# A row softmax on one core: an unrolled, framework-synchronised schedule rewritten with hand-made semaphores and hardware loops

## The chip, the cores and the metric

The kernel runs on one core of one Trainium2 chip. The engines that matter here are DVE (VectorE), ACT (ScalarE), Pool (GpSimd), SP (SyncE), PE's sequencer (no matrix work is done) and the core's 16 DMA engines. The metric is the device time of one execution in microseconds. A "span" is the time from the first to the last instruction in the profiled execution; it is about 1.8 us shorter than the time of the same execution. P below means the time from the first instruction of one tile to that of the next on DVE.

## The reference

```python
batch, seq, dim = 32, 512, 1024        # x: float32, temperature: 0.5
scaled  = x / temperature
shifted = scaled - np.max(scaled, axis=-1, keepdims=True)
exp_x   = np.exp(shifted)
out     = exp_x / np.sum(exp_x, axis=-1, keepdims=True)
```

These are 16384 rows of 1024 numbers: 67.1 MB in and 67.1 MB out. A tile is 128 partitions times 8 rows, 4 MB, and there are 16 tiles.

## The kernel before

Six tile buffers. SP loads, Pool stores, and a buffer is loaded again when its store has landed. The work goes in groups of 4 rows of a partition, two groups a tile. The framework makes the semaphores, and everything is unrolled.

```python
def maximum(g):      # DVE: row maxima of 4 rows, then bias = -scale * max
    nc.vector.tensor_reduce(out=top, in_=tiles[i][:, a : a + k, :], ..., op=extreme)
    nc.vector.tensor_scalar_mul(bias, in0=top, scalar1=-scale)

def exponential(g):  # ACT: exp(scale * x + bias) in place, and the sum of each row
    for b in range(k):
        nc.scalar.activation(tiles[i][:, a + b, :], tiles[i][:, a + b, :], Exp,
                             bias=bias[:, b : b + 1], scale=scale, accum_out=sums[:, b : b + 1])

def divide(g):       # DVE: 1 / sum, then one multiply a row
    nc.vector.reciprocal(recip, sums)
    for b in range(k):
        nc.vector.tensor_scalar_mul(...)
# ... cut ...
with tc.manual_schedule():
    for _ in range(BUFS):
        load()
    for g in range(len(groups) + 1):
        if g < len(groups):
            maximum(g)
            exponential(g)
        if g > 0:
            divide(g - 1)       # one group late
            store(g - 1)        # a 4 MB store at the end of each tile; then load()
```

While ACT does the exponentials of group g, DVE divides group g - 1 and then reduces group g + 1.

## Time and profile before

318.23 us, median of 3 runs (318.2 to 318.88).

| | before |
|---|---|
| span of the profiled execution | 316.9 us |
| DVE busy, ACT busy | 235.5 us, 149.6 us |
| DMA rate, 40 to 280 us | 432 to 434 GB/s |
| tile to tile (P), steps two to five / from the seventh on | 14.8 / 19.4 us (one of 20.2) |
| table loads on ACT | 1 |

The page of the kernel before. Each digit is a fortieth of the span, 7.9 us, in tenths busy; GB/s is what the DMA engines moved in it.

```profile
span 316.9 us, 639 instructions
DVE 235.5 (74%) x224; ACT 149.6 (47%) x257; POOL 8.8 (3%) x20
DVE  0399999999689494995949869496793967949710
DMA  8999999999999999999999999999999999999995
GB/s 331 409 451 414 385 459 422 438 436 422 455 405 455 409 459 405 455 422 438 434 426 451 409 455 411 455 414 447 426 434 435 426 451 409 451 418 447 430 414 232
```

The DMA row is full from the second slice to the last but one. DVE is full only at the start, while the six tiles loaded first are worked off; afterwards it has holes. The view of waits of the same kernel says what these holes are (engine, line, who was waited for: us in total, times, longest):

```profile
ACT xt L79 <- DVE recip L91: 119.5, 25, 8.1
DVE top L70 <- DMA xt<-in_x_dram: 62.8, 12, 13.1
DVE recip L91 <- ACT xt L79: 2.1, 2, 1.9
```

DVE's reduce waited 12 times for a load, and DVE waited almost never for ACT (2.1 us). The timeline of the second tile shows why (DVE's lines, and ACT's first exponential of the tile; the rest left out): the reciprocal at 29.84 works on the sums of the group before, which are long there.

```profile
25.31 4.41 DVE L70 TENSOR_REDUCE top<-xt 128x4 f32<-128x4096 f32 x1
29.76 0.17 DVE L73 TENSOR_SCALAR bias<-top 128x4 f32<-128x4 f32 x1
29.84 0.17 DVE L91 RECIPROCAL recip<-sums 128x4 f32<-128x4 f32 x1
29.96 1.15 ACT L79 ACTIVATE xt<-xt,bias 128x1024 f32<-128x1024 f32 x1 [3.03 <-DVE bias L73]
30.04 2.74 DVE L93 TENSOR_SCALAR xt<-xt,recip 128x1024 f32<-128x1024 f32 x4
32.70 4.41 DVE L70 TENSOR_REDUCE top<-xt 128x4 f32<-128x4096 f32 x1
```

So DMA bounds this kernel, and DVE and ACT have slack in every tile. First Pool's issue of the last two stores (the timeline: start us, us), then the DMA view of 280 to 325 us, each digit 1.1 us:

```profile
290.65 0.53 POOL L101 DMA_DIRECT2D out_dram<-xt  x1 [18.82 <-DVE xt L93]
302.90 0.53 POOL L101 DMA_DIRECT2D out_dram<-xt  x1 [11.72 <-DVE xt L93]
```

```profile
DMA  9999989989999999999859999999640000000000
GB/s 437 437 437 466 466 350 408 437 379 437 408 466 466 466 437 437 437 466 466 350 233 466 466 466 437 466 466 466 291 204 29 0 0 0 0 0 0 0 0 0
```

The last store is issued while the one before it is still moving, so the rate dips in one slice (233 GB/s) but no hole opens until the bytes are used up. By the landings in the trace, the last four stores end at 286.5, 296.1, 305.8 and 315.5 us: 9.7 us each, the time of 4 MB at the 432 to 434 GB/s of the middle.

Last, two lines of the page's groups (busy us, mean ns; idle before them):

```profile
L79 ACT ACTIVATE xt<-xt,bias 128x1024 f32<-128x1024 f32 x128 | 145.4, 1137 | 136.9 <-DVE recip L91 119.5
L79 ACT ACT_TABLE_LOAD x1 | 1.3, 1283 | 13.2 <-DMA xt<-in_x_dram 13.2
```

ACT loads the table of the exponential once, at the start, while DVE makes the first reduce.

### The profile page before, as it was taken

The page shows a single profiled execution, that of the slowest core. Times are in us where ns is not written, and L with a number is a line of the kernel's source. Part 1 is how long each engine was busy: PE and PEld are TensorE (multiplying, and loading weights), DVE is VectorE, ACT ScalarE, POOL GpSimd, SP SyncE. Part 2 cuts the span into 40 slices and gives each one's busy share as a digit, 9 for nine tenths or more (in the row PEclk, how much of TensorE's full clock was granted, in tenths as well). Part 3 has the DMA queues.
Part 4 walks back from the last instruction along what each step waited for, and adds up shares of the span by engine and source line. Part 5 has one row for each costly group of instructions (what it writes and reads, how often), then busy time and mean ns, then how long its engine had stood idle before and what let it go on. Part 6 is the DMA issues. An engine that isn't in the chain of part 4 may idle for free.

```text
span 316.9 us, 639 instructions
## 1 busy us (share of the span) xinstructions
DVE 235.5 (74%) x224; ACT 149.6 (47%) x257; POOL 8.8 (3%) x20
## 2 busy tenths in 40 slices
DVE  0399999999689494995949869496793967949710
ACT  0176666666526255361554606455163551635500
POOL 0000000000000000000000000000000000000000
DMA  8999999999999999999999999999999999999995
GB/s 331 409 451 414 385 459 422 438 436 422 455 405 455 409 459 405 455 422 438 434 426 451 409 455 411 455 414 447 426 434 435 426 451 409 451 418 447 430 414 232
DMA packets 4612, 134.25 MB, mean 424 GB/s; under 512 B 512, under 2 KB 512, under 8 KB 512
## 3 DMA queue, kind: packets, MB, share of 16 engines
q1 hardware_dynamic: 2304, 67.11, 49.5%
q0 software_dynamic: 2304, 67.11, 49.1%
q14 instruction: 4, 0.03, 0.0%
HBM read 67.11 MB, written 67.11 MB: 424 GB/s over the span
## 4 chain that ended last, share of the span: by engine, by line
issue 89%; DMA 4%; POOL 2%; POOLq 0%
DMA xt<-in_x_dram 4%; POOL out_dram L101 2%; POOLq L147 0%; POOLq L101 0%
## 5 line engine op out<-in xcount | busy, mean ns | idle before, releaser
L79 ACT ACTIVATE xt<-xt,bias 128x1024 f32<-128x1024 f32 x128 | 145.4, 1137 | 136.9 <-DVE recip L91 119.5
L70 DVE TENSOR_REDUCE top<-xt 128x4 f32<-128x4096 f32 x32 | 141.3, 4416 | 62.8 <-DMA xt<-in_x_dram 62.8
L93 DVE TENSOR_SCALAR xt<-xt,recip 128x1024 f32<-128x1024 f32 x128 | 87.7, 749 | 1.1
L79 ACT ACTIVATION_READ_ACCUMULATOR xt<-xt,bias 128x1 f32 x128 | 23.8, 186 | 0.0
L101 POOL DMA_DIRECT2D out_dram<-xt x16 | 8.6, 540 | 294.4 <-DVE xt L93 294.4
L79 ACT ACT_TABLE_LOAD x1 | 1.3, 1283 | 13.2 <-DMA xt<-in_x_dram 13.2
L91 DVE RECIPROCAL recip<-sums 128x4 f32<-128x4 f32 x32 | 5.5, 171 | 2.1 <-ACT xt L79 2.1
L73 DVE TENSOR_SCALAR bias<-top 128x4 f32<-128x4 f32 x32 | 5.4, 170 | 1.1
L133 POOL MEMSET const-float32-0.0<- 128x1 f32 x1 | 0.1, 98 | 0.2 <-issue 0.2
L133 POOL MEMSET const-bfloat16-1.0<- 128x1 bf16 x1 | 0.1, 101 | 0.0
L133 POOL MEMSET const-float32-1.0<- 128x1 f32 x1 | 0.1, 98 | 0.0
L133 POOL MEMSET const-uint8-127<- 128x1 uint8 x1 | 0.1, 98 | 0.0
## 6 DMA issues: line engine op xcount, KB each, us to landing
xt<-in_x_dram SPq DMA_DIRECT2D x16, 4096.0 KB, 50.2
out_dram<-xt POOLq DMA_DIRECT2D x16, 4096.0 KB, 38.4
```

Source lines behind the costliest of these rows:

```text
L70: nc.vector.tensor_reduce(out=top, in_=tiles[i][:, a : a + k, :], axis=mybir.AxisListType.X, op=extreme)
L73: nc.vector.tensor_scalar_mul(bias, in0=top, scalar1=-scale)
L79: nc.scalar.activation(tiles[i][:, a + b, :], tiles[i][:, a + b, :], mybir.ActivationFunctionType.Exp, bias=bias[:, b : b + 1], scale=scal ...
L91: nc.vector.reciprocal(recip, sums)
L93: nc.vector.tensor_scalar_mul(tiles[i][:, a + b, :], in0=tiles[i][:, a + b, :], scalar1=recip[:, b : b + 1])
L101: nc.gpsimd.dma_start(out=dram(of, i)[:, a : a + k, :], in_=tiles[i][:, a : a + k, :])
L133: nc = _bacc.Bacc("TRN2", target_bir_lowering=False, num_devices=1)
```

## The change

The intent: make the semaphores by hand, and let DVE and ACT loop over the tiles instead of being unrolled. Slot addresses come from registers. SP only loads, Pool only stores, and PE's idle sequencer counts landings in order. The diff, cut to its core:

```diff
-TILES = [[8]] * 16
-BUFS = 6
+SLOTS, ROWS = 6, 8
...
+    def take(engine, sem, count=1):
+        engine.wait_ge(sem, count).then_inc(sem, -count)
...
-    with tc.manual_schedule():
-        for g in range(len(groups) + 1):
-            ...            # maximum(g), exponential(g), divide(g - 1), store(g - 1)
+    with tc.tile_critical():
+        # SP: wait for stored[slot], load.  Pool: wait for scaled, store.
+        for i in range(tiles):
+            nc.tensor.wait_ge(loaded[i % SLOTS], 16 * (i // SLOTS + 1)).then_inc(ready, 1)
...
+        with nc.vector.Fori(0, tiles) as t:
+            first = t % SLOTS * ROWS
+            take(nc.vector, ready)
+            for a in starts:                               # 0, 4
+                nc.vector.tensor_reduce(out=top[...], in_=ring[:, bass.ds(first + a, GROUP), :],
+                    ...).then_inc(topped, 1)
+                take(nc.vector, topped)
+                nc.vector.tensor_scalar_mul(bias[...], in0=top[...], scalar1=-scale
+                    ).then_inc(biased, GROUP)
+            for a in starts:
+                take(nc.vector, summed, GROUP)
+                nc.vector.reciprocal(recip[...], sums[...]).then_inc(inverted, 1)
+                take(nc.vector, inverted)
+                for b in range(a, a + GROUP):
+                    row = ring[:, bass.ds(first + b, 1), :]
+                    ins = nc.vector.tensor_scalar_mul(row, in0=row, scalar1=recip[:, b : b + 1])
+                ins.then_inc(scaled, 1)
+
+        with nc.scalar.Fori(0, tiles) as t:
+            first = t % SLOTS * ROWS
+            for b in range(ROWS):
+                row = ring[:, bass.ds(first + b, 1), :]
+                if b in starts:
+                    take(nc.scalar, biased, GROUP)
+                nc.scalar.activation(row, row, Exp, bias=bias[:, b : b + 1], scale=scale,
+                    accum_out=sums[:, b : b + 1]).then_inc(summed, 1)
...
+    with tc.tile_critical():
+        nc.sync.wait_ge(stored[...], ...)                  # the last store
```

DVE no longer divides one group late: within a tile it reduces twice and then divides twice. Every `take` of DVE and ACT is an instruction of its own, which waits and also subtracts: in the trace of the kernel after one starts on DVE 0.11 us in front of the bias, which comes 0.15 us after the end of the reduce. And nobody writes the load of ACT's table: whoever builds the program puts it in front of the first exponential, and that now stands inside a loop, behind the wait for the bias.

More of the change, by code (lines that the diff above doesn't have):

```diff
@@ L32 @@
     n, d = xf.shape
-    assert sum(sum(ks) for ks in TILES) * P == n
-    data = ctx.enter_context(tc.tile_pool(name="data", bufs=BUFS))
-    stats = ctx.enter_context(tc.tile_pool(name="stats", bufs=4))
-    groups, first, r = [], [], 0
-    for i, ks in enumerate(TILES):
-        first.append(r)
-        r += sum(ks)
-        a = 0
-        for k in ks:
-            for b in range(0, k, GROUP):
-                m = min(GROUP, k - b)
-                groups.append((i, a + b, m, (a, k) if b + m == k else None))
-            a += k
@@ L50, in dram @@
-    def dram(t, i):
-        k = sum(TILES[i])
-        block = t[P * first[i] : P * (first[i] + k), :]
-        return block.rearrange("(p k) d -> p k d", p=P, k=k)
-    tiles, small = [], []
-    def load():
-        i = len(tiles)
-        if i < len(TILES):
-            xt = data.tile([P, sum(TILES[i]), d], f32, name="xt")
-            nc.sync.dma_start(out=xt, in_=dram(xf, i))
-            tiles.append(xt)
-    def maximum(g):
-        i, a, k, _ = groups[g]
-        top, bias, sums, recip = (
-            stats.tile([P, k], f32, name=name) for name in ("top", "bias", "sums", "recip")
-        )
-        small.append((bias, sums, recip))
-        nc.vector.tensor_reduce(
-            out=top, in_=tiles[i][:, a : a + k, :], axis=mybir.AxisListType.X, op=extreme
-        )
-        nc.vector.tensor_scalar_mul(bias, in0=top, scalar1=-scale)
@@ L75, in exponential @@
-    def exponential(g):
-        i, a, k, _ = groups[g]
-        bias, sums, _ = small[g]
-        for b in range(k):
-            nc.scalar.activation(
-                tiles[i][:, a + b, :],
-                tiles[i][:, a + b, :],
-                mybir.ActivationFunctionType.Exp,
-                bias=bias[:, b : b + 1],
-                scale=scale,
-                accum_out=sums[:, b : b + 1],
-            )
-    def divide(g):
-        i, a, k, _ = groups[g]
-        _, sums, recip = small[g]
-        nc.vector.reciprocal(recip, sums)
-        for b in range(k):
-            nc.vector.tensor_scalar_mul(
-                tiles[i][:, a + b, :], in0=tiles[i][:, a + b, :], scalar1=recip[:, b : b + 1]
-            )
@@ L97, in store @@
-    def store(g):
-        i, _, _, part = groups[g]
-        if part:
-            a, k = part
-            nc.gpsimd.dma_start(out=dram(of, i)[:, a : a + k, :], in_=tiles[i][:, a : a + k, :])
-            if a + k == sum(TILES[i]):
-                load()
-    with tc.manual_schedule():
-        for _ in range(BUFS):
-            load()
-        for g in range(len(groups) + 1):
-            if g < len(groups):
-                maximum(g)
-                exponential(g)
-            if g > 0:
-                divide(g - 1)
-                store(g - 1)
+    tiles = n // (P * ROWS)
@@ new lines @@
+    assert tiles * P * ROWS == n and ROWS % GROUP == 0
+    starts = range(0, ROWS, GROUP)
+    pool = ctx.enter_context(tc.tile_pool(name="data", bufs=1))
+    ring = pool.tile([P, SLOTS * ROWS, d], f32, name="ring")
+    top = pool.tile([P, ROWS], f32, name="top")
+    bias = pool.tile([P, ROWS], f32, name="bias")
+    sums = pool.tile([P, ROWS], f32, name="sums")
+    recip = pool.tile([P, ROWS], f32, name="recip")
+    loaded = [tc.alloc_semaphore(f"loaded{s}") for s in range(SLOTS)]
+    stored = [tc.alloc_semaphore(f"stored{s}") for s in range(SLOTS)]
@@ new lines, with slot @@
+    ready, topped, biased, summed, inverted, scaled = (
+        tc.alloc_semaphore(name)
+        for name in ("ready", "topped", "biased", "summed", "inverted", "scaled")
+    )
+    def dram(t, i):
+        return t[P * ROWS * i : P * ROWS * (i + 1), :].rearrange("(p k) d -> p k d", p=P, k=ROWS)
+    def slot(i):
+        s = i % SLOTS
+        return ring[:, ROWS * s : ROWS * (s + 1), :]
+    def take(engine, sem, count=1):
+        engine.wait_ge(sem, count).then_inc(sem, -count)
+    with tc.tile_critical():
+        for i in range(tiles):
+            if i >= SLOTS:
+                nc.sync.wait_ge(stored[i % SLOTS], 16 * (i // SLOTS))
+            nc.sync.dma_start(out=slot(i), in_=dram(xf, i)).then_inc(loaded[i % SLOTS], 16)
+        for i in range(tiles):
+            nc.tensor.wait_ge(loaded[i % SLOTS], 16 * (i // SLOTS + 1)).then_inc(ready, 1)
+        for i in range(tiles):
+            nc.gpsimd.wait_ge(scaled, len(starts) * (i + 1))
+            nc.gpsimd.dma_start(out=dram(of, i), in_=slot(i)).then_inc(stored[i % SLOTS], 16)
+        with nc.vector.Fori(0, tiles) as t:
+            first = t % SLOTS * ROWS
+            take(nc.vector, ready)
+            for a in starts:
+                nc.vector.tensor_reduce(
+                    out=top[:, a : a + GROUP],
+                    in_=ring[:, bass.ds(first + a, GROUP), :],
+                    axis=mybir.AxisListType.X,
+                    op=extreme,
+                ).then_inc(topped, 1)
+                take(nc.vector, topped)
+                nc.vector.tensor_scalar_mul(
+                    bias[:, a : a + GROUP], in0=top[:, a : a + GROUP], scalar1=-scale
+                ).then_inc(biased, GROUP)
+            for a in starts:
+                take(nc.vector, summed, GROUP)
+                nc.vector.reciprocal(
+                    recip[:, a : a + GROUP], sums[:, a : a + GROUP]
+                ).then_inc(inverted, 1)
+                take(nc.vector, inverted)
[9 more added lines that the diff above has]
+                    take(nc.scalar, biased, GROUP)
+                nc.scalar.activation(
+                    row,
+                    row,
+                    mybir.ActivationFunctionType.Exp,
+                    bias=bias[:, b : b + 1],
+                    scale=scale,
+                    accum_out=sums[:, b : b + 1],
+                ).then_inc(summed, 1)
+        for i in range(tiles - SLOTS, tiles - 1):
+            nc.sync.wait_ge(stored[i % SLOTS], 16 * (i // SLOTS + 1))
@@ L120 @@
+    with tc.tile_critical():
+        nc.sync.wait_ge(
+            stored[(tiles - 1) % SLOTS],
+            16 * ((tiles - 1) // SLOTS + 1),
+            synchronizes=[nc.sync.lower_ap(slot(tiles - 1))],
+        )
 _INS = ['x', 'temperature']
```

## The prediction

> **What bounds the kernel now.** The DMA engines. In the table of windows they are 100% busy and move 432 to 434 GB/s in every window from 40 to 300 us, while DVE is busy about 75% and ACT about 50%. [...] 134.2 MB at 433 GB/s is 310 us; the first load is issued at 0.74 us and lands at 13.1. By the landings the last four stores end 9.65 us apart (286.5, 296.1, 305.8, 315.5): store 15 is issued at 302.9, while store 14 runs, so even the tail has no gap. DVE's 62.8 us of waiting for loads (view of waits) is slack.
>
> **What the change does.** Loads, stores, slots and data instructions stay. What differs:
> 1. DVE no longer works on the previous group during the exponentials. Per tile the order is reduce, reduce, divide four, divide four, and the second divide waits for ACT's eighth exponential. From durations in the timeline: reduce 4.42 + bias 0.17, then eight exponentials at 1.13 from start to start (9.1), reciprocal 0.17, four multiplies 2.65 until the next reduce can start: 16.7 us, plus about five separate semaphore instructions on the chain at 0.06 each (an event-semaphore instruction of DVE or ACT stands 0.06 us before the instruction behind it in this trace), plus registers: P = 17.1 us a tile, against 14.76 now in the compute-bound start (13 to 77 us) and 19.36 for the DMA.
> 2. Loop control: [...] It should hide under DVE's four queued multiplies (2.7 us).
> 3. The table load (1.28 us, once now, hidden behind the first reduce). If it lies in ACT's loop behind the wait for the bias, it is on each tile's chain: P = 18.3 to 18.5.
> 4. Landing goes through PE: about 0.1 us, visible only when DVE waits.
> 5. Start and end: section entry may cost tenths; most of the nine semaphore instructions behind the last landing (0.55 us) go.
>
> **Critical path.** Almost none of it. Compute bounds the kernel only if 13.5 + 16 P passes about 303.5 us, where store 15 would leave a gap behind store 14: P above 18.1. Below that the time stays; above it each 0.1 us of P costs 1.6 us. With P near 17.1 there is 1 us a tile to spare; with the table load in the loop, P = 18.3 to 18.5 costs 3 to 7 us.
>
> **Prediction.** 318.4 us, 8 in 10 between 317.0 and 323.5. Faster by over 2%: 0.01; within 2%: 0.86; slower by over 2%: 0.13.
>
> **What would show it.** Right: DMA still at 433 GB/s in all middle slices; the first store issued earlier than 33.1 us (about 31), the next ones 17 to 18 us apart (14.8 now) until DVE begins to wait for loads, then 19.4; ACT's share unchanged or up by 16 table loads (20 us); last stores landing 9.65 us apart. Wrong: DMA digits under 9 in the middle, stores over 18.1 us apart to the end, DVE waiting for ACT and not for loads.
>
> **What would make it wrong.** Register-addressed instructions that cannot be queued ahead, so that each multiply or exponential pays for its address; a table load a tile with more than 1.3 us behind it; [...] multiplies losing their 0.66 us rate; section entry and exit costing microseconds.

## The result, and the profile after

326.23 us, median of 6 runs (326.17 to 326.32), against 318.24 for the kernel before in the same rounds. The ratio is 1.0248, 95% interval 1.0235 to 1.0261. A ratio here is the mean time of one kernel's fast runs over that of the other's of the same rounds, so not quite the ratio of the medians quoted. The change is slower by 8 us, and outside the predicted range.

The page of the kernel after, the same lines:

```profile
span 324.5 us, 1109 instructions
DVE 238.4 (73%) x224; ACT 167.1 (52%) x272; POOL 8.8 (3%) x20
DVE  0377959787895969788795978789596978879520
DMA  8999999999999899999999999999999999999466
GB/s 323 416 428 448 388 452 404 436 452 412 428 452 452 388 452 452 404 436 452 420 420 452 448 400 444 448 408 436 448 428 416 448 452 404 436 452 412 174 259 259
```

The middle is as full as before. What differs is in the last three slices. Pool's last two stores and the DMA view of 280 to 325 us:

```profile
292.27 0.53 POOL L73 DMA_DIRECT2D out_dram<-ring  x1 [18.02 <-DVE ring L97]
310.83 0.53 POOL L73 DMA_DIRECT2D out_dram<-ring  x1 [18.02 <-DVE ring L97]
```

```profile
DMA  9996899899999999988880000000999999966000
GB/s 466 466 466 291 350 437 408 379 466 466 466 466 466 466 466 466 466 350 350 350 350 29 0 0 0 0 0 0 466 466 466 466 466 466 408 262 262 0 0 0
```

A hole of some 7 us: the DMA engines have nothing left to move from about 305 to 312 us, because the last tile is not yet divided. By the landings, store 14 ends at 305.5 us and store 15 at 322.2, which is 16.7 us apart instead of 9.7. The rest of the loss stands behind the last landing: 2.28 us to the end of the span, against 1.45 before.

So the question is why DVE comes late to the last tile. The timeline of one tile in the middle, DVE and then ACT, cut to lines that bear on the chain (start us, us; in brackets the idle time before):

```profile
143.45 4.41 DVE L79 TENSOR_REDUCE top<-ring 128x4 f32 x1
148.01 0.17 DVE L86 TENSOR_SCALAR bias<-top 128x4 f32<-128x4 f32 x1
154.82 2.74 DVE L97 TENSOR_SCALAR ring<-ring,recip  x4
159.01 0.18 DVE L91 RECIPROCAL recip<-sums 128x4 f32<-128x4 f32 x1 [1.46 <-DVEq L61]
159.34 2.74 DVE L97 TENSOR_SCALAR ring<-ring,recip  x4 [0.15 <-DVEq L61]
162.00 4.41 DVE L79 TENSOR_REDUCE top<-ring 128x4 f32 x1
```

```profile
148.41 1.28 ACT L106 ACT_TABLE_LOAD   x1 [8.10 <-ACTq L61]
149.71 1.15 ACT L106 ACTIVATE ring<-ring,bias  x1
157.65 1.13 ACT L106 ACTIVATE ring<-ring,bias  x1
158.68 0.19 ACT L106 ACTIVATION_READ_ACCUMULATOR ring<-ring,bias 128x1 f32 x1
```

This is a serial chain: reduce (143.45), bias (148.01), table load (148.41), eight exponentials (149.71 to 158.87), reciprocal (159.01), four multiplies (159.34), and then the next tile's reduce at 162.00. P is 18.56 us, and the trace shows it in all 15 steps (18.55 to 18.57). Nothing in it waits for a load, which the view of waits of the kernel after confirms ("DVEq L61" is DVE's own sequencer, standing in the `take` on line 61):

```profile
DVE recip L91 <- DVEq L61: 49.0, 32, 1.6
DVE top L79 <- DVEq L61: 13.6, 1, 13.6
```

The reduce, which waited 12 times before, now waits once, for the very first load. Instead the reciprocal waits 32 times, for ACT's sums. And the table load is there 16 times, behind the wait for the bias:

```profile
L106 ACT ACT_TABLE_LOAD x16 | 20.5, 1283 | 140.0 <-ACTq L61 140.0
```

One more thing is to be read from these numbers. P is 18.56 us, less than the 19.4 us that DMA needs for a tile's load and store, and still compute sets the end. With six slots the loads run ahead: at the start DMA moves loads only (the first store is issued at 32.5 us), and the stores that it owes are moved last. What counts is the last store alone, which is issued at about 13.5 + 16 P + 0.4 us. A store issued when nothing else moves lands 11.35 us later (310.83 to 322.18), and in the runs below in which DMA sets the end the last landing is at 314.9 to 315.1 us. So a last store issued before about 303.7 us queues behind store 14 and nothing is lost. That gives a knee, the P at which the time begins to rise, at 18.1, an estimate from these landings and issue times.

### The profile page after: what moved, and what is told of

Its sections match the earlier page's. It is cut to its first block, busy times and chain, and to the rows that moved or that the text cites. A ratio compares the mean times of both kernels' runs of the same rounds, so it can differ in the third digit from the quotient of the medians.

```text
span 324.5 us, 1109 instructions
## 1 busy us (share of the span) xinstructions
DVE 238.4 (73%) x224; ACT 167.1 (52%) x272; POOL 8.8 (3%) x20
## 5 line engine op out<-in xcount | busy, mean ns | idle before, releaser
L79 DVE TENSOR_REDUCE top<-ring 128x4 f32 x32 | 141.3, 4416 | 13.6 <-DVEq L61 13.6
L106 ACT ACTIVATE ring<-ring,bias x128 | 145.1, 1134 | 0.2
L106 ACT ACT_TABLE_LOAD x16 | 20.5, 1283 | 140.0 <-ACTq L61 140.0
L97 DVE TENSOR_SCALAR ring<-ring,recip x128 | 87.7, 748 | 4.8 <-DVEq L61 0.5
L106 ACT ACTIVATION_READ_ACCUMULATOR ring<-ring,bias 128x1 f32 x128 | 23.8, 186 | 0.0
L73 POOL DMA_DIRECT2D out_dram<-ring x16 | 8.6, 540 | 302.3 <-DVE ring L97 302.3
```

The source lines that it names most:

```text
L73: nc.gpsimd.dma_start(out=dram(of, i), in_=slot(i)).then_inc(stored[i % SLOTS], 16)
L79: nc.vector.tensor_reduce(out=top[:, a : a + GROUP], in_=ring[:, bass.ds(first + a, GROUP), :], axis=mybir.AxisListType.X, op=extreme,).th ...
L97: ins = nc.vector.tensor_scalar_mul(row, in0=row, scalar1=recip[:, b : b + 1])
L106: nc.scalar.activation(row, row, mybir.ActivationFunctionType.Exp, bias=bias[:, b : b + 1], scale=scale, accum_out=sums[:, b : b + 1],).th ...
```

## The experiments

Theory A: the time follows from P, the serial chain of a tile. The table load behind the wait is on that chain, and it lifts P above 18.1. Theory B: loop control, register addresses and separate semaphore instructions are what costs, and the table loads fall into time in which ACT is idle anyway. In all the profiles DMA moved the same 134.2 MB.

| kernel | table loads | P while compute bounds, us | last store issued, us | time, us | ratio to before, 95% interval |
|---|---|---|---|---|---|
| after | 16 | 18.56 | 310.8 | 326.23 | 1.0235 to 1.0261 |
| e1_preload | 1 | 17.41 | 301.6 | 319.07 | 1.0015 to 1.0043 |
| e2_load_early | 16, in front of the wait | 17.41 | 301.5 | 319.07 | 1.0015 to 1.0046 |
| e7_pipelined | 16 | 15.50 | 300.4 | 319.25 | 1.0021 to 1.0052 |
| d1024 | 1 | 18.19 | 305.0 | 320.39 | 1.0058 to 1.0089 |
| d3072 | 1 | 20.26 | 338.4 | 353.65 | 1.1091 to 1.1125 |
| e5_unrolled_loads | 16 | 18.43 | 308.6 | 324.14 | 1.0169 to 1.0200 |
| e6_counts_loads | 16 | 18.07 | 303.0 | 319.16 | 1.0017 to 1.0047 |
| e8_one_section | 1 | 15.50 | 301.5 | 319.60 | 1.0031 to 1.0059 |

The outputs are right. P and the issue times are read from each kernel's profile.

### e1_preload: the table loaded once, ahead of the loop

```diff
+        nc.scalar.preload_act_table(mybir.ActivationFunctionType.Exp)
         with nc.scalar.Fori(0, tiles) as t:
```

> The changed kernel with the exponential's table loaded once, ahead of ACT's loop. Theory A (the table load of 1.28 us, which stands in ACT's loop behind the wait for the bias, lengthens each tile's chain; compute then passes the 18.1 us a tile at which the DMA stops hiding it): tiles 17.26 us apart while compute bounds, then DVE waits for loads and the DMA is at 433 GB/s in the middle; 319.2 us, the 1 us over the kernel before being the entry and exit of the hand-made sections. Theory B (loop control, register addresses and separate semaphore instructions are what slows it; the loads are incidental, one more thing on an idle ACT): about 326 us as in the changed kernel, tiles still about 18.5 us apart.

319.07 us. With the table loaded ahead, the load in the loop is gone. P fell to 17.41, and after ten tiles DVE catches up with the loads and waits for them again. The view of waits of e1_preload:

```profile
DVE recip L91 <- DVEq L61: 30.7, 32, 1.6
DVE top L79 <- DVEq L61: 22.2, 6, 13.5
```

The reduce waits 6 times, five of them after the first load, as in a kernel bound by DMA. All of the loss but 1 us is gone with one line, while loops, registers and separate semaphore instructions are all still there. Theory B in its plain form falls. The P of 17.41 is 0.15 above the expectation of 17.26: without the load, ACT is through its first four exponentials by the time that the second bias reaches it. The timeline of e1_preload's first tile shows it:

```profile
22.78 0.17 DVE L86 TENSOR_SCALAR bias<-top 128x4 f32<-128x4 f32 x1
22.96 0.19 ACT L107 ACTIVATION_READ_ACCUMULATOR ring<-ring,bias 128x1 f32 x1
23.16 1.15 ACT L107 ACTIVATE ring<-ring,bias  x1
```

The fifth exponential starts 0.20 us after the start of the read of the fourth sum; the others follow such a read by 0.09. In the kernel after, where ACT runs later, the fifth follows by 0.09 as well (24.28 to 24.38 us), so the expected 17.26, which is that kernel's P without the load (18.56 less 1.30), did not hold this wait.

### e2_load_early: the same 16 loads, in front of the wait

```diff
         with nc.scalar.Fori(0, tiles) as t:
+            nc.scalar.preload_act_table(mybir.ActivationFunctionType.Exp)
             first = t % SLOTS * ROWS
```

> The changed kernel with the table load moved in front of the wait for the bias, still one in each turn of ACT's loop: 16 loads stay, ACT's busy time stays near 167 us. Theory A, where only the place of the load on the chain counts: 17.26 us a tile, 319.2 us. A theory that the number of table loads or ACT's busy time costs: 326 us. Theory B: 326 us.

319.07 us, the same as e1. ACT still makes 16 loads. The timeline of ACT in e2_load_early shows where one of them went:

```profile
27.60 0.19 ACT L107 ACTIVATION_READ_ACCUMULATOR ring<-ring,bias 128x1 f32 x1
27.80 1.28 ACT L101 ACT_TABLE_LOAD   x1
35.90 1.15 ACT L107 ACTIVATE ring<-ring,bias  x1 [6.81 <-ACTq L61]
```

It runs right behind the last exponential of the tile before, in the 8 us in which ACT waits for the next bias. So neither the number of loads nor ACT's busy time (20.5 us of loads here and in the kernel after) costs anything in this kernel. What costs is the place behind the wait.

### e7_pipelined: the loads left in place, DVE in the old order

```diff
+        take(nc.vector, ready)
+        maximum(0, 0)
+        with nc.vector.Fori(0, tiles - 1) as t:
+            first = t % SLOTS * ROWS
+            maximum(first, GROUP)
+            divide(first, 0)
+            take(nc.vector, ready)
+            maximum((t + 1) % SLOTS * ROWS, 0)
+            divide(first, GROUP)
+        # the last tile's rest behind the loop
```

> The changed kernel with the table loads left where they are (16, behind the wait), but DVE in the order of the kernel before: it reduces one group while ACT does the exponentials of the group before, and divides one group late, across the loop's edge. Theory A: each tile's DVE work of about 15.4 us (14.76 plus separate semaphore instructions) with ACT's 10.6 us beside it, nothing serial, so below 18.1 us a tile and back to the DMA bound: 319.2 us. If the loads slow something else (theory that ACT_TABLE_LOAD costs by itself): 326 us. Theory B: 326 us, since loop, registers and semaphores stay.

319.25 us, P 15.50. With the order of the kernel before, DVE has work while ACT loads its table and does exponentials, and the load costs nothing although it is 16 times behind the wait. So the table load and the serial order are both needed for the loss. Neither alone brings P above the knee.

### d1024 and d3072: ordinary work in the place of the load

The table is loaded ahead, and exponentials of 1024 columns into a spare buffer stand behind the wait, once (d1024) or three times (d3072) a tile.

```diff
                     take(nc.scalar, biased, GROUP)
+                    if b == 0:
+                        for r in range(3):                  # d1024: range(1)
+                            nc.scalar.activation(spare[:, 1024 * r : 1024 * (r + 1)],
+                                bias[:, 0:1].to_broadcast([P, 1024]), Exp, bias=bias[:, 0:1], scale=scale)
```

> The table loaded once ahead of the loop as in e1_preload, and in its place an exponential of 1024 columns into a spare buffer that nobody reads, behind the wait for the bias once a tile: about 1.04 us on the chain, no table load. Theory A, where any microsecond at that place counts: 17.26 + 1.04 = 18.3 us a tile, so 16 x 0.2 = 3.2 us above the DMA bound of 319.2: 322.4 us. A theory that table loads as such cost: 319.2 us. Theory B: 326 us.

> As d1024, with three exponentials of 1024 columns at that place instead of one. Each adds 1.04 us to the chain (d1024 measured 18.19 us a tile): 20.27 us a tile. Theory A with its slope of 16 us for each us a tile: last store issued at 338.3 us, landed 11.35 us later, 353.7 us in all. If DMA and compute trade off softly, less than that.

d1024 took 320.39 us at P = 18.19, and d3072 353.65 us at P = 20.26. Theory A's number for d1024 was 322.4, too high because P came out 0.1 lower than added up. The trace shows where: in the kernel after, a register operation of 0.11 us for the row's address stands between ACT's wait and its table load, and bias to load takes 0.42 us (18.12 to 18.54). The spare exponential has a fixed address, and bias to exponential takes 0.30 (18.16 to 18.46); that the register operation falls behind its start is the author's explanation. For d3072, built on the P that d1024 showed, 353.7 was expected. Table loads as such are therefore not the cause; work of another kind at that place does the same. The DMA view of 280 to 352 us of d3072 shows what the end looks like when compute bounds it throughout (each digit 1.8 us):

```profile
DMA  9896600000696976000006696960000009696900
```

A hole now stands in front of each of the last three stores, which land 20.3 us apart.

### e5_unrolled_loads and e6_counts_loads: loops off, then separate waits off

e5 writes the loops out 16 times (static addresses) and keeps one table load a tile behind the wait:

```diff
-        with nc.vector.Fori(0, tiles) as t:
+        for t in range(tiles):
...
-        with nc.scalar.Fori(0, tiles) as t:
+        for t in range(tiles):
...
                     take(nc.scalar, biased, GROUP)
+                    if b == 0:
+                        nc.scalar.preload_act_table(mybir.ActivationFunctionType.Exp)
```

> No loop and no register addresses: DVE's and ACT's turns are written out 16 times, with the same separate semaphore instructions, the same order, and one table load a tile at the same place behind the wait for the bias. Theory A (the load on the chain): of the 18.56 us a tile only the register operation between ACT's wait and its table load goes, about 0.1 us, so 18.45 us a tile and 324.4 us. Theory B in the form that the loop and its register addresses cost the time: DMA bound again, 319.1 us.

e6 is e5 with semaphores that only count up, so that the next instruction can carry the wait itself:

```diff
+    seen = {}
     def take(engine, sem, count=1):
-        engine.wait_ge(sem, count).then_inc(sem, -count)
+        seen[sem.name] = seen.get(sem.name, 0) + count
+        engine.wait_ge(sem, seen[sem.name])
```

> As e5_unrolled_loads, but the semaphores count up for ever, so that the instructions carry their waits themselves and the separate wait-and-subtract instructions go. In the trace of the changed kernel these hops take 0.15 us (reduce to bias), 0.24 (bias to table load), 0.15 (sums to reciprocal), 0.15 (reciprocal to multiply) against 0.03 each in the kernel before: about 0.45 us a tile less. Theory A with these hops as the second part: 18.0 us a tile, just under the knee of 18.1, so about 319.2 us with 16 table loads still on the chain. If the separate semaphore instructions cost nothing: as e5, 324.4 us.

e5 took 324.14 us at P = 18.43, as Theory A expected: the loops and register addresses together cost 0.13 us a tile, nearly all of it the register operation in front of the table load. e6 took 319.16 us at P = 18.07: the separate waits cost another 0.36 us a tile. The timeline of e6's first tile shows shorter hops on the same chain:

```profile
13.43 4.42 DVE L81 TENSOR_REDUCE top<-ring 128x4 f32<-128x4096 f32 x1 [13.43 <-PEq L72]
17.96 0.17 DVE L88 TENSOR_SCALAR bias<-top 128x4 f32<-128x4 f32 x1
18.15 1.28 ACT L109 ACT_TABLE_LOAD   x1 [18.15 <-DVE bias L88]
19.45 1.15 ACT L110 ACTIVATE ring<-ring,bias 128x1024 f32<-128x1024 f32 x1
```

From the start of the bias to that of the table load it is 0.19 us here, 0.28 in e5 (17.92 to 18.20) and 0.40 in the kernel after. (The bias starts 0.11 us after the end of the reduce, against 0.15 in the kernel after and 0.03 in the kernel before.) So theory B holds a part of the truth: 0.49 of the 18.56 us are loop and semaphore costs, and without them the table loads just fit under the knee. Both parts count only because their sum passes it. From d1024 to d3072 the time rises by 33.26 us for 2.08 us of P, 16 us for each us; below the knee, from 15.5 to 18.07 us, it stays between 319.1 and 319.6.

### e8_one_section: a try for a better version

Table ahead, pipelined order, and the last wait moved into the first hand-made section:

```diff
-        for i in range(tiles - SLOTS, tiles - 1):
+        for i in range(tiles - SLOTS, tiles):
             nc.sync.wait_ge(stored[i % SLOTS], 16 * (i // SLOTS + 1))
-    with tc.tile_critical():
-        nc.sync.wait_ge(stored[(tiles - 1) % SLOTS], ...)
```

> A try for a better version: table loaded ahead of the loop, DVE in the pipelined order of e7_pipelined, and the last wait moved into the one hand-made section, so that the second section falls away. Compute is hidden; the DMA bound leaves only the ends. The end after the last landing took 1.45 us in the kernel before and 2.28 us in the changed one; without the second section about 1.8 us, so 318.7 us, still not under the kernel before (318.1). If the excess of 1 us is not at the ends but in the middle: 319.2 us as in e7_pipelined.

319.60 us: a miss, and worse than with two sections. The last landing is at 315.0 us and the span ends at 317.6, so the end is 2.6 us long instead of the expected 1.8. In its trace the author read that Pool's drain instruction at the section's end starts only after SP has seen the last landing, and takes 1.36 us from there. In the kernels before and after it has begun before (at 302.88 and 310.81 us) and ends 0.70 us after the landing. No version tried beats the kernel before. With compute hidden, the end behind the last landing is 2.28 us in each of the other rewritten kernels, against 1.45 before, and the first load is issued 0.2 us later: together the 1 us that they stay above it. No run took these ends away, so that sum is read from traces and not tested.

## Why the prediction was wrong

The step that failed is item 3 of the prediction, where it stood between two values of P. It took the table load to be off the tile's chain and built its time on P = 17.1; the load was on the chain in each of the 16 tiles, and P was 18.56, above the knee that it had worked out itself. The terms one by one:

- "The DMA engines bound the kernel now, even the tail has no DMA gap": right.
- "Compute bounds the kernel only ... P above 18.1; above it each 0.1 us of P costs 1.6 us": right. d1024 at 18.19 is just above the knee, e6 at 18.07 just below, and the slope measured 16 us for each us.
- "P = 17.1 us a tile" without a table load in the loop: e1 measured 17.41. (The durations listed add up to 16.5, not to the 16.7 given.) The term that was too small is the separate semaphore instruction, put at 0.06 us. On the chain a hop took 0.15 us (reduce to bias) or 0.24 (end of the bias to the table load), against 0.03 where an instruction carries its own wait. e5 against e6 gives 0.36 us a tile for all of them. The wait for the second bias, 0.11 in e1, was not in the sum.
- "If it lies in ACT's loop behind the wait for the bias ... P = 18.3 to 18.5": this step failed, by being treated as an unlikely case. It was the case: 16 loads, P = 18.56, and the range's upper end of 323.5 and the 13% for "slower" stood on the other one. The trace before could have warned: there the load stood right in front of the first exponential, but not behind the wait for the bias, which the exponential carried itself. With `take` that wait became an instruction ahead of the load. The trace before has no loop, so it did not show how often a load in one runs; this kernel's trace does, with 16 loads, one in each turn. (Which tool placed the load no run shows.)
- "With the table load in the loop ... 3 to 7 us": measured 8.0. P was 0.06 above the upper value, which makes 1 us over 16 tiles, and the ends came on top.
- "Start and end: section entry may cost tenths; most of the nine semaphore instructions ... go": wrong in sum. The first load is issued 0.2 us later (0.94 against 0.74), and the end behind the last landing is 0.83 us longer (2.28 against 1.45), with two sections and handshakes between engines in place of the nine waits. Nor were the nine there to be saved: in both kernels Pool's drain instruction ends 0.70 us after the last landing, and before, the nine were done by then (315.98, against 316.15). From the drain to the end of the span it is 0.76 us before and 1.59 after. e1, e2, e6 and e7, in which compute is hidden, are 0.9 to 1.2 us above the kernel before of the same rounds by their medians.
- "Landing goes through PE: about 0.1 us", the author's estimate: too low. From the first landing to the reduce it is 0.38 us (13.17 to 13.55) against 0.02 (13.09 to 13.12). Spread over 16 tiles the difference is 0.02 us of P, so the knee hardly moves.
- "The first store issued earlier than 33.1 us (about 31), the next ones 17 to 18 us apart until DVE begins to wait for loads": e1 does this (31.3 us, 17.4 apart). The kernel after has 32.5 us and 18.6 apart to the end, which the prediction had named as the sign of being wrong.

The loss of 8 us adds up from the two profiles: the last landing is 6.7 us later (322.18 against 315.45), and the end behind it 0.83 us longer, together 7.56 us, the difference of the spans. The profiled execution of the kernel before took 318.68 us, 0.44 above the median, and that is the rest.

## What to carry to other kernels

When a schedule is rolled into a loop, look at what the tools put into the loop's body for you, above all a table load in front of the first activation. Loading the table once ahead of the loop, or at the top of the body in front of the first wait, made it free here (319.07 us in e1 and in e2). Under a DMA bound, work out the knee, the per-tile time of the serial chain at which the last store comes too late. This kernel passed it by 0.46 us a tile and lost 7 us against e1, while the DMA row stayed full almost everywhere. An order that lets an engine work on the neighbouring group kept the addition off the chain here (e7: 16 loads behind the wait, P 15.50, 319.25 us), and should not be given up for a tidier loop body.

## Single instructions, as the traces show them

- A load of ACT's table took 1283 ns in the kernels before and after, e1, e2, e6, e7 and d3072. In the kernel after, where the same table is loaded again in each turn, the exponential behind the load started 1.30 us after the load's start (148.41 to 149.71), with nothing added.
- The load behind the wait in the loop ran once a turn (16 in the kernel after, 20.5 us of ACT). With the table loaded ahead of the loop, none ran in it (e1: 1 load).
- The compare-and-branch on DVE was recorded with 56 ns, and the next instruction started 0.19 us after its start (159.862 to 160.053 us in the kernel after), hidden under multiplies already queued (159.34 to 162.08).
- After a semaphore wait that also subtracts, as an instruction of its own, the next DVE instruction started 0.11 us later (kernel after), against 0.06 after a plain wait instruction in the kernel before. On the chain it made a hop of 0.15 us, where an instruction that carries its own wait took 0.03.
- Pool's drain at the end ended 0.70 us after the last store's landing in the kernels before and after, where it had begun before that landing. In e8 the author read 1.36 us for one that began after it. Why it differs stays open.
